# Second step of the Fourier stage: standing operands in two halves, two stores requested by ScalarE, a table load and two clears at later places

## The chip, the cores and the metric

The kernel runs on one core of a Trainium2 chip. The core has five engines with a queue of instructions each: TensorE (PE; its weight loads are listed as PEld), VectorE (DVE), ScalarE (ACT), GpSimd (POOL) and SyncE (SP, which here does little but request DMA transfers). Sixteen DMA engines move data. The metric is the time of one execution on the device in microseconds (us); the time of the kernel before is 973.52 us, the median of three runs (971.64 to 975.0).

## The reference

An encoder layer is applied to two sequences of 1024 columns, 256 and 2048 tokens long, with the same weights. Cut to what matters:

```python
def fourier_mix(u, w_f, b_f):                  # 8 groups of 64 columns
    ug = u.reshape(b, s, F_GROUPS, F_GROUP_DIM)
    spec = jnp.fft.fft2(ug, axes=(1, 3), norm='ortho')
    return spec.real.reshape(b, s, F_WIDTH) @ w_f + b_f

def encoder_layer(x, ...):
    h = rms_norm(x, g_pre)
    q, k, v, z_a, u_f, z_f = split(h @ w_in)   # six times 512 columns
    y_a = neighbourhood_attention(q, k, v, rpb)
    y_f = fourier_mix(u_f, w_f, b_f)
    mixed = concat([rms_norm(y_a, g_na) * silu(z_a),
                    rms_norm(y_f, g_f) * silu(z_f)])
    return x + rms_norm(mixed @ w_out, g_post)
```

The whole is in float32. A matrix product that needs the accuracy is made of three products of split operands, a high part and a low part (names that end in `h` and `l`); the split is a cast of the operand and a subtraction of the cast from it.

## The kernel before, in words

**Stages.** The projections come first. Their last and longest part is a loop `for i in range(16)` over pairs of output blocks, each with seven products `mm` on TensorE (lines 164 to 166). For the `z` columns the result `f` gets a silu on ScalarE (line 882) and is stored to `zD` (line 883), two stores of 512 KB for a pair. The loop's last pair, `i == 15`, is such a pair. During it SyncE also loads the constants `d2` and the first twelve `zg` tiles (line 831), the results of the Fourier stage's first step, which lie in `ZD` in DRAM.

**The Fourier stage's second step** follows (lines 982 to 1080). It runs in four rounds `gq`, each over five tiles `c`. A round reads four `zg` loads of 256 KB. Tiles 0 to 3 are `pab` products with a standing operand of 128 columns (a slice of `zg`) and 64 moving columns of `d2`, four products for a tile; tile 4 has three stripes of 32 columns side by side. In round 0 each tile has a product with one moving column as well (`pny`), and in round 2 one for the 256-token sequence (`pup`, from the loads `up` and `f256`). In the trace a float32 product is two records, so a full `pab` tile shows as eight. `split_ab` splits each result: the cast (`abh`, `a`) is on ScalarE, or on VectorE for tiles 0 to 2 of round 0, and the subtraction (`abl`) on VectorE. `pab` uses three PSUM buffers: tags `b` (two) and `c` (one). After round 2 comes a first pass `pq(0)` and after round 3 a second, `pq(1)`, and `pq32`: products `ppq` of `cs2`, `c32` with the load `wf` (1 MB), split into `pqh`, `pql` and `w32`.

**Y.** Then `py` products (lines 164 to 166 and 1263) make the mixed columns in four blocks `e`, each in three parts. ScalarE adds the bias (line 1268), VectorE combines two PSUM tiles into `Y` (line 1276) and SyncE stores `Y` (line 1302 the 256-token part, line 1325 the other, 1 MB). `Y` has two buffers, so the third block's first combination needs the first block's stores landed. Attention over the loads `kl`, `ql`, `v` and the biases `tb`, the norms, and the output projection with the weights `wo` make up the rest. `kh` is the cast of `kl` (line 1095, ScalarE), and `za` a small load of `zD` (line 1159).

**Order.** Up to `man.close()` (line 976) and for TensorE everywhere the order of the instructions is written by hand. From line 977 to the third block of `Y` a scheduler sets the order of the other engines by the waits that it foresees; `issue_after(x)` holds an instruction until `x` has been placed. Each engine then runs its queue strictly in that order.

**DMA lanes.** A request tells its completion on one of eight semaphores, `DMAHW0` to `DMAHW7` in the rows below. They are taken in turn over all requests of SyncE and ScalarE, and before a request goes out its engine waits until the last transfer of the same lane has landed.

**Small parts that the change touches.** The activation table load (line 978) follows the last silu. The clears of `ptb` (line 992), two PSUM tiles that attention uses later, open the stage on VectorE. `norm_sums` copies sums of squares out of PSUM into `nsb` on ScalarE (line 1481), eight times between 630 and 858 us.

Of the kernel before, what the change touches and what calls it, by code (L numbers as in the profile page):

```python
# [10 lines left out]
F32 = mybir.dt.float32  # L11
F32R = mybir.dt.float32r
AF = mybir.ActivationFunctionType
ALU = mybir.AluOpType
# [154 lines left out]
def build(tc, A, O):  # L169
    nc = tc.nc  # L170
# [10 lines left out]
    zD = dr.tile([2, 512, T], F32, name="zD")  # L181
# [23 lines left out]
    dnyq = cst.tile([128, 2], F32, name="dnyq")  # L205
# [11 lines left out]
    def mmt(n):  # L217
        x = mmc[0] % 5 > 2
        mmc[0] += 1
        return ps.tile([128, n], F32, tag="t" if x else "a", name="mm", bufs=2 if x else 3)  # L220
# [10 lines left out]
    def gt(shape, dtype, name):  # L231
        return gp.tile(shape, dtype, tag="g", name=name)
# [293 lines left out]
    def pair(i):  # L526
        return i if i < 8 else 15 - i
# [190 lines left out]
    for c in range(3, 6):  # L718
# [7 lines left out]
        if c == 4:  # L726
# [5 lines left out]
            for k in range(KC):  # L732
                for t in range(2):
                    ts = slice(128 * t, 128 * t + 128)
                    nc.vector.scalar_tensor_tensor(out=xp[:, k, ts], in0=xs[t][:, k], scalar=gpre[:, k:k + 1],
                                                   in1=ivb[0][:, ts], op0=ALU.mult, op1=ALU.mult)
# [23 lines left out]
    for b in range(16):  # L760
        kind, blk = divmod(b, 4)
# [12 lines left out]
        if 2 <= b < 8:  # L774
            x, y = divmod(b, 2)
# [7 lines left out]
        p = mmt(512)[:, :TP]  # L783
# [3 lines left out]
        o = st.tile([128, 256], F32, tag="f", name="f", bufs=3)  # L787
        if kind % 2:
            i, d = p, o
        else:  # L790
            i = p.rearrange("p (b r c) -> p b r c", b=2, c=32)
# [43 lines left out]
    def load_d(j):  # L835
        return load([128, 8, 128], A["d2"][:, 8 * j:8 * j + 8, :], "d2")

    zgs = []
    for i in range(16):
# [14 lines left out]
        kind, blk = divmod(2 * pair(i), 4)  # L854
        o = [st.tile([128, 1024], F32, tag="f", name="f", bufs=3) for x in range(2)]
# [23 lines left out]
        def store(f):  # L879
            ts = slice(TP + 1024 * sg, TP + 1024 * sg + 1024)  # L880
            if kind < 2:
                silu_[0] = nc.scalar.activation(o[f], o[f], AF.Silu)
                nc.sync.dma_start(zD[kind, (blk + f) * 128:(blk + f) * 128 + 128, ts], o[f])
            else:
                nc.sync.dma_start((kD if kind == 2 else qD)[blk + f, :, ts], o[f])

        silu_ = [None]
        for j in range(7):
            if i in (0, 8):
                if j in (0, 3):  # L890
# [27 lines left out]
            if sg == 0:  # L918
                x, y = divmod(7 * (pr - 1) + j, 14)
# [17 lines left out]
            for f, d in ((u_load, 0), (u_split, 4), (u_stage1, 6)):  # L937
                x = 7 * pr + j - 7 - d
# [4 lines left out]
            if i == 15 and j in (1, 3, 4, 5):  # L943
                if j == 1:
                    d2 = [load_d(0), load_d(1)]
# [4 lines left out]
            p = mmt(512)  # L950
# [5 lines left out]
            if j == 0:  # L956
                nc.scalar.copy(e_("u0"), p)
            elif j == 1:
                comb(0, 0, "u0", p)
            elif j == 2:  # L960
                add("u2", "u0")
            elif j == 3:
                add("u4", "u2")
            elif j == 4:
                comb(1, 1, "u4", p)
                add("u3", "u2")
            elif j == 5:
                comb(1, 0, "u3", p, ALU.subtract)
                store(1)
            else:  # L970
                comb(0, 1, "u4", p)
                store(0)
        if kind < 2:
            silu = silu_[0]

    man.close()
    with tc.issue_after(silu.ins):
        nc.scalar.preload_act_table_set("natural_log_exp_and_others")
    ph.close()


# [6 lines left out]
    sqs = sqp.tile([128, T], F32, name="sqs")  # L988
    ab = pf.enter_context(tc.tile_pool(name="ab", bufs=1))
    ptb = [ps.tile([128, 512], F32, tag="t", name="ptb", bufs=2) for i in range(2)]  # L990
    for x in ptb:
        nc.vector.memset(x, 0.0)
    pg = ExitStack()
    sm = pg.enter_context(tc.tile_pool(name="smF", bufs=1))
    f256 = sm.tile([128, 2, 258], F32, name="f256")
# [16 lines left out]
    a32 = ab.tile([96, NCOL], F32R, name="a32")  # L1012
    AC = [[x[:, c % 2] for x in AB[c // 2]] for c in range(4)]

    def split_ps(dh, dl, src, vec=False):
        nc.vector.tensor_copy(dh, src) if vec else nc.scalar.copy(dh, src)
        nc.vector.tensor_tensor(out=dl, in0=src, in1=dh.bitcast(F32), op=ALU.subtract)

    def dft(p, c, pairs):
        sts = [(p[32 * r:32 * r + 32], slice(256, 512, 8)) for r in range(3)] if c == 4 else \  # L1020
            [(p, slice(c * 128, c * 128 + 128))]
        for out, cols in sts:
            for x, (z, d) in enumerate(pairs):
                nc.tensor.matmul(out, z[:, cols], d, start=x == 0, stop=x == len(pairs) - 1)  # L1024


    def split_ab(gq, c, view, p):
        if c < 4:
            split_ps(view(AC[c][0]), view(AC[c][1]), p, gq == 0 and c < 3)
        else:  # L1030
            nc.scalar.copy(view(a32), p)
            lo = view(a32[64:96])
            nc.vector.tensor_tensor(out=lo, in0=p[64:96], in1=lo.bitcast(F32), op=ALU.subtract)

    def stage2(gq, zg, c):
        m = int(c in (2, 3))
        np_ = 96 if c == 4 else 128
        x = (gq * 5 + c) % 3 == 2
        p = ps.tile([np_, 4, 64], F32, tag="c" if x else "b", name="pab", bufs=1 if x else 2)
        for g in range(4):  # L1040
            dft(p[:, g, :], c, [(zg[g], d2[gq // 2][:, (gq % 2) * 4 + g, m * 64:m * 64 + 64])])
        split_ab(gq, c, lambda a: a[:, :1024].rearrange("p (k q g l) -> p q g k l", k=16, q=4, g=4)[:, gq],
                 p.rearrange("p g (k l) -> p g k l", l=4))
        if gq == 0:
            p = ps.tile([np_, 1], F32, tag="a", name="pny")
            dft(p, c, [(zg[0], dnyq[:, m:m + 1])])
            split_ab(gq, c, lambda a: a[:, 1024:1025], p)
        if gq == 2:
            p = ps.tile([np_, 129], F32, tag="a", name="pup")
            dft(p, c, [(up[:, t], f256[:, t, 129 * m:129 * m + 129]) for t in range(2)])  # L1050
            split_ab(gq, c, lambda a: a[:, 1025:1154], p)
# [4 lines left out]
    def pq(m):  # L1056
        h = gt([128, 2, 512], F32R, "pqh")
        l = gt([128, 2, 512], F32R, "pql")
        for c in range(2):
            p = ps.tile([128, 512], F32, tag="a", name="ppq")  # L1060
            for x in range(2):
                nc.tensor.matmul(p[64 * x:64 * x + 64], cs2[:, m, :], wf[:, 2 * c + x, :], start=True, stop=True)  # L1062
            split_ps(h[:, c], l[:, c], p)
        PQ.append((h, l))

    def pq32():
        p = ps.tile([96, 512], F32, tag="a", name="ppq")
        for c in range(4):
            nc.tensor.matmul(p, c32[:, c], wf[:, c], start=c == 0, stop=c == 3)
        nc.scalar.copy(w32, p)  # L1070
        nc.vector.tensor_tensor(out=w32[32:64], in0=p[32:64], in1=w32[32:64].bitcast(F32), op=ALU.subtract)

    for gq in range(4):
        for c in range(5):
            stage2(gq, zgs[gq], c)
        if gq == 2:
            pq(0)
    pq(1)
    pq32()
    pg.close()  # L1080
# [163 lines left out]
    for t, (g, x) in enumerate(zip(G, (0, 640))):  # L1244
        g["w"] = []
        for c0, w in g["t"]:
            n = 2 * g["nr"] * w
# [67 lines left out]
    for e in range(4):  # L1315
        Y = sqy.tile([128, T], F32, tag="Y", name="Y", bufs=2)
        if e < 3:
# [10 lines left out]
            for i in range(T // SQ if e < 2 else 1):  # L1328
                ts = slice(i * SQ, i * SQ + SQ)
# [146 lines left out]
    def norm_sums(sq, ts):  # L1476
        n = 32 * len(ts)
        for x, t in enumerate(ts):
            nc.tensor.matmul(ptb[0][32 * x:32 * x + 32, :128], ones32, sq[:, t * 128:t * 128 + 128], start=True, stop=True)
        o = sm.tile([128, 128], F32, name="nsb", bufs=1)[:n]  # L1480
        nc.scalar.copy(o, ptb[0][:n, :128])  # L1481
        nsb.append(o)

    def norm_turn(dst, ts):
# [89 lines left out]
    for k in range(2, len(G) + 1):  # L1574
        pr, i = divmod(k, 9)
        g, f = G[k] if k < len(G) else None, G[k - 1] if k else None
# [19 lines left out]
        x = k // 2 + 1  # L1596
# [52 lines left out]
        if k + 1 in NT:  # L1649
            norm_sums(sqs if k < 31 else ysq, NT[k + 1])  # L1650
# [8 lines left out]
        if 32 <= k < 36:  # L1659
            x, d = k - 32, atiles[k - 32]  # L1660
# [122 lines left out]
```

## Time and profile before

| | |
|---|---|
| median of three runs | 973.52 us (971.64 to 975.0) |
| the profiled execution | 970.48 us, of which the span of instructions is 968.7 us |
| granted TensorE clock in it | 0.998 |
| busy share | PE 99%, PEld 83%, DVE 73%, ACT 51%, POOL 44% |
| DMA | 279.89 MB, mean 289 GB/s |
| second step of the Fourier stage | from 549 us (first `pab`) to 576.6 us (first `py`) |

Times of the trace are microseconds from the start of the span. A row of the timeline has the start, the duration, engine, line, operation, tiles written and read, their shape and the number of merged instructions, and in brackets how long the engine stood idle before and what ended that. In a group of the profile, "busy, mean ns" are followed by the idle time before the group's instructions and what ended it. The profile's DMA share is the mean busy share of the sixteen engines. The busy share of PE counts matmuls whose ends are modelled, so 99% says that it always had something under way, not that it was at its peak.

### The profile page before, as it was taken

How to read it: one execution, taken by the hardware profiler on the slowest of the kernel's cores; microseconds unless marked ns; L12 is line 12 of the kernel's file. 1: busy time of each engine (PE TensorE's matmuls, PEld its weight loads, DVE VectorE, ACT ScalarE, POOL GpSimd, SP SyncE). 2: the span in 40 equal slices, each digit the busy share in tenths (PEclk: the TensorE clock that was granted, in tenths of full speed). 3: DMA queues.
4: the chain of work that ended last, by engine and by line, in shares of the span. 5: the costliest groups of instructions: out<-in, count | busy, mean ns of one | idle time of the engine just before them, and what ended most of it. 6: DMA issues, size and time to landing. Idle time of an engine off the chain costs nothing.

```text
span 968.7 us, 17031 instructions
## 1 busy us (share of the span) xinstructions
PE 958.9 (99%) x5769; PEld 801.0 (83%) x5769; DVE 709.5 (73%) x1306; ACT 497.5 (51%) x1078; POOL 430.2 (44%) x400
## 2 busy tenths in 40 slices
PE   9999999999999999999999999999999999999997
PEld 7889988888888888888888879887788888878886
DVE  6768987777986867787777446776665656649997
ACT  6836675433325533333344255677666776744443
POOL 3100003464752202756654033577677686624544
PEclk9999999999999999999999999999999999999999
DMA  9899696556849996599989898698887998979993
GB/s 327 312 373 357 234 366 240 194 189 252 318 163 377 352 410 239 211 371 320 322 303 339 301 328 300 210 281 273 258 240 234 286 327 270 296 244 331 330 346 129
DMA packets 146450, 279.89 MB, mean 289 GB/s; under 512 B 13162, under 2 KB 84284, under 8 KB 142972
## 3 DMA queue, kind: packets, MB, share of 16 engines
q1 hardware_dynamic: 145932, 278.41, 82.4%
q8 instruction: 46, 0.75, 0.3%
q10 hardware_dynamic: 432, 0.39, 0.1%
q14 instruction: 40, 0.33, 0.1%
HBM read 184.37 MB, written 101.72 MB: 295 GB/s over the span
## 4 chain that ended last, share of the span: by engine, by line
PE 96%; DVE 1%; ACT 1%; issue 1%; POOL 1%; DMA 0%; DVEq 0%; SPq 0%; POOLq 0%; ACTq 0%
PE po L1432 19%; PE mm L165 18%; PE mm L164 18%; PE mm L166 18%; PE pv L1521 5%; PE ptb L1505 5%; PE s L1181 4%; PE pab L1024 2%; PE py L164 1%; PE py L166 1%; PE py L165 1%; DMA gpre<-gpre 0%; PE ppq L1062 0%; PE pz L166 0%; PE pz L164 0%
## 5 line engine op out<-in xcount | busy, mean ns | idle before, releaser
L164 PE MATMUL mm<-xh,wa 128*128 128x512 f32 x448 | 174.4, 389 | 0.0
L165 PE MATMUL mm<-xl,wa 128*128 128x512 f32 x448 | 174.3, 389 | 0.0
L166 PE MATMUL mm<-xh,wa 128*128 128x512 f32 x448 | 174.3, 389 | 0.0
L536 POOL TENSOR_TENSOR ws<-wr 128x512 f32<-128x512 f32 x16 | 22.2, 1386 | 226.6 <-DMA wr<-wz 222.8
L1215 POOL TENSOR_SCALAR w<-w,m 128x480 f32<-128x480 f32 (+6 forms) x136 | 86.0, 644 | 46.3 <-DVE m L1212 35.9
L164 PEld LDWEIGHTS mm<-xh,wa 128*128 128x128 f32 x448 | 84.1, 188 | 17.6
L166 PEld LDWEIGHTS mm<-xh,wa 128*128 128x128 f32 x448 | 84.1, 188 | 17.5
L165 PEld LDWEIGHTS mm<-xl,wa 128*128 128x128 f32 x448 | 84.1, 188 | 17.4
L1432 PE MATMUL po<-wo,yh 128*128 128x512 f32 x272 | 90.4, 413 | 0.0
L551 DVE TENSOR_TENSOR wa<-wr,wa 128x512 fp32r<-128x512 f32 x60 | 68.5, 1149 | 27.1 <-ACT wa L550 26.8
L1208 ACT ACTIVATE w<-w,m 128x480 f32<-128x480 f32 (+6 forms) x136 | 79.3, 586 | 17.1 <-DVE m L1203 17.1
L1432 PE MATMUL po<-w,yh 128*128 128x512 f32 x280 | 86.7, 391 | 0.0
L1203 DVE CUSTOM_DVE_ANT_1 w<-s,tb 128x360 f32<-128x360 f32 (+5 forms) x124 | 62.4, 541 | 10.3 <-PE s L1181 9.8
L589 POOL TENSOR_TENSOR mt<-mt,rmask 128x880 f32<-128x880 f32 (+2 forms) x24 | 51.0, 2139 | 34.1 <-DVE mt L585 27.6
L165 PE MATMUL mm<-vl,xh 128*128 128x512 f32 x168 | 65.5, 390 | 0.2 <-DVE vl L482 0.2
L164 PE MATMUL mm<-vh,xh 128*128 128x512 f32 x168 | 65.4, 389 | 0.0
L166 PE MATMUL mm<-vh,xl 128*128 128x512 f32 x168 | 65.4, 389 | 0.0
L877 DVE TENSOR_TENSOR f<-u,mm 128x512 f32<-128x512 f32 x64 | 43.5, 680 | 28.0 <-PE mm L166 23.1
L1432 PEld LDWEIGHTS po<-w,yh 128*128 128x128 f32 x280 | 52.3, 188 | 10.9 <-issue 0.2
L1505 PE MATMUL ptb<-ident,w 128*120 128x128 f32 (+5 forms) x428 | 59.5, 276 | 1.0 <-ACT nsb L1481 0.9
L550 ACT CAST wa<-wr 128x512 fp32r<-128x512 f32 x60 | 36.4, 617 | 44.1 <-PE mm L166 23.2
L1521 PEld LDWEIGHTS pv<-pt,v 120*64 120x64 f32 (+6 forms) x896 | 48.2, 136 | 12.8 <-issue 9.6
(263 smaller groups left out, 2394.3 us busy)
## 6 DMA issues: line engine op xcount, KB each, us to landing
wr<-wz SPq DMA_DIRECT2D x48, 512.0 KB
vl<-sD SPq DMA_DIRECT2D x20, 512.0 KB
xm<-xm SPq DMA_DIRECT2D x9, 1024.0 KB
oD<-ofs SPq DMA_DIRECT2D x18, 512.0 KB
of<-oD SPq DMA_DIRECT2D x18, 512.0 KB
yr<-yD SPq DMA_DIRECT2D x34, 256.0 KB
zD<-f SPq DMA_DIRECT2D x16, 512.0 KB
woD<-wo SPq DMA_DIRECT2D x16, 512.0 KB
```

What stands on the lines that cost most here:

```text
L164: nc.tensor.matmul(out, lh, rh, start=first, stop=False)
L165: nc.tensor.matmul(out, lh, rl, start=False, stop=False)
L166: nc.tensor.matmul(out, ll, rh, start=False, stop=last)
L551: nc.vector.tensor_tensor(out=o[:, 1], in0=src, in1=o[:, 0].bitcast(F32), op=ALU.subtract)
L589: nc.gpsimd.tensor_tensor(out=o, in0=i, in1=rmask[:, m0:m0 + n].unsqueeze(2).to_broadcast([128, n, 80]), op=ALU.add)
L877: nc.vector.tensor_tensor(out=dst(f, b), in0=src(uu[u]), in1=src(p), op=op)
L1203: nc.vector.tensor_tensor_reduce(out=rows(g["w"][b][:, h, :n], w), in0=rows(g["s"][2 * b + h][:, :n], w), in1=tv, scale=1.0, scalar=3.0e38 ...
L1208: nc.scalar.activation(w, w, AF.Exp, bias=m[:, h:h + 1], scale=-1.0, accum_out=m[:, 2 + h:3 + h])
L1215: nc.gpsimd.tensor_scalar(w, w, m[:, 4 + h:5 + h], 1.0, ALU.mult, ALU.mult)
L1432: nc.tensor.matmul(p, (d["l"] if x == 2 else d["h"])[:, c], w(n, int(x == 1), c), start=j == 0, stop=j == 11)
L1505: nc.tensor.transpose(ptb[h][:nk, j * 128:j * 128 + 128], g["w"][b][:, h, c0:c0 + nk], ident)
L1521: nc.tensor.matmul(p[hs, b], g["v"][:nk, v, hs], g["pt"][b][:nk, h, j * 128:j * 128 + 128], start=j == 0, stop=j == len(ch) - 1)
```

## The change

Six edits, the first four in the title:

1. `dft` takes a width `w`. The `pab` and `pny` products of tiles 0 to 3 are called with 64: each standing operand of 128 columns becomes two halves of 64 columns, one after the other in the program, that write partitions 0 to 63 and 64 to 127. `pup` and tile 4 stay.
2. For `i == 15` the two stores to `zD` are requested by ScalarE, behind each silu, not by SyncE.
3. The table load moves from behind the last silu to behind the last ScalarE cast of round 3.
4. The two clears of `ptb` move to the end of round 1.
5. The cast of tile 2 in round 0 moves from VectorE to ScalarE.
6. The copy to `nsb` moves from ScalarE to VectorE.

```diff
         def store(f):
             if kind < 2:
-                silu_[0] = nc.scalar.activation(o[f], o[f], AF.Silu)
-                nc.sync.dma_start(zD[kind, (blk + f) * 128:(blk + f) * 128 + 128, ts], o[f])
+                nc.scalar.activation(o[f], o[f], AF.Silu)
+                q = nc.scalar if i == 15 else nc.sync
+                q.dma_start(zD[kind, (blk + f) * 128:(blk + f) * 128 + 128, ts], o[f])
...
     man.close()
-    with tc.issue_after(silu.ins):
-        nc.scalar.preload_act_table_set("natural_log_exp_and_others")
...
     ptb = [ps.tile([128, 512], F32, tag="t", name="ptb", bufs=2) for i in range(2)]
-    for x in ptb:
-        nc.vector.memset(x, 0.0)
...
-    def dft(p, c, pairs):
-        sts = [(p[32 * r:32 * r + 32], slice(256, 512, 8)) for r in range(3)] if c == 4 else \
-            [(p, slice(c * 128, c * 128 + 128))]
+    def dft(p, c, pairs, w=128):
+        if c == 4:
+            sts = [(p[32 * r:32 * r + 32], slice(256, 512, 8)) for r in range(3)]
+        else:
+            sts = [(p[r:r + w], slice(c * 128 + r, c * 128 + r + w)) for r in range(0, 128, w)]
...
-            split_ps(view(AC[c][0]), view(AC[c][1]), p, gq == 0 and c < 3)
+            split_ps(view(AC[c][0]), view(AC[c][1]), p, gq == 0 and c < 2)
...
-            dft(p[:, g, :], c, [(zg[g], d2[gq // 2][:, (gq % 2) * 4 + g, m * 64:m * 64 + 64])])
+            dft(p[:, g, :], c, [(zg[g], d2[gq // 2][:, (gq % 2) * 4 + g, m * 64:m * 64 + 64])], 64)
...
-            dft(p, c, [(zg[0], dnyq[:, m:m + 1])])
+            dft(p, c, [(zg[0], dnyq[:, m:m + 1])], 64)
...
     for gq in range(4):
         for c in range(5):
             stage2(gq, zgs[gq], c)
+        if gq == 1:
+            with tc.issue_after(last["dve"].ins):
+                for x in ptb:
+                    nc.vector.memset(x, 0.0)
         if gq == 2:
             pq(0)
+        if gq == 3:
+            with tc.issue_after(last["act"].ins):
+                nc.scalar.preload_act_table_set("natural_log_exp_and_others")
...
-        nc.scalar.copy(o, ptb[0][:n, :128])
+        nc.vector.tensor_copy(o, ptb[0][:n, :128])
```

**How the order changes on SyncE**, from the twelve `zg` loads on (tile numbers tell the pairs of loads apart; `zg_4771` and `zg_4774` are round 1's, `zg_4793` and `zg_4796` round 2's). Before:

```order
L831 DMA zg_4771<-ZD_70 128x512 [waits DMAHW6_49,PE_49]
L831 DMA zg_4771<-ZD_70 128x512
L831 DMA zg_4774<-ZD_70 128x512 [waits DMAHW0_49]
L831 DMA zg_4793<-ZD_70 128x512 [waits DMAHW2_49,PE_49]
L831 DMA zg_4796<-ZD_70 128x512 [waits DMAHW5_49]
L883 DMA zD_69<-f_4694 128x1024 [waits DMAHW6_49,Activation_49]
L883 DMA zD_69<-f_4693 128x1024 [waits DMAHW7_49,Activation_49]
L996 DMA f256_4859<-f256 128x516 [waits DMAHW0_49,PE_49]
L998 DMA up_4861<-uD_71 128x2x512 [waits DMAHW1_49]
```

and now:

```order
L831 DMA zg_4771<-ZD_70 128x512 [waits DMAHW0_49,PE_49]
L831 DMA zg_4771<-ZD_70 128x512 [waits DMAHW1_49]
L831 DMA zg_4774<-ZD_70 128x512 [waits DMAHW2_49]
L831 DMA zg_4793<-ZD_70 128x512 [waits DMAHW4_49,PE_49]
L831 DMA zg_4796<-ZD_70 128x512 [waits DMAHW7_49]
L989 DMA f256_4856<-f256 128x516 [waits DMAHW0_49,PE_49]
L991 DMA up_4858<-uD_71 128x2x512 [waits DMAHW1_49]
```

The two stores are gone from this queue, and the lanes have moved: in the program's new order the first store takes lane 1 and the second lane 4 ahead of the loads shown, so the second load of `zg_4771` (the sixth of twelve) waits on lane 1 for the first store, and the first load of `zg_4793` (the ninth) on lane 4 for the second.

**ScalarE at the same place.** Before:

```order
L882 ACTIVATE f<-f 128x1024 [waits DMAHW4_49,DVE_49,Activation_49]
L882 ACTIVATE f<-f 128x1024 [waits DMAHW0_49,DVE_49]
L978 ACT_TABLE_LOAD
L1016 CAST abh_4877<-pny 128x1 [waits PE_49]
L1031 CAST a_4879<-pab 96x4x16x4 [waits PE_49]
```

and now:

```order
L882 ACTIVATE f<-f 128x1024 [waits DMAHW4_49,DVE_49,Activation_49]
L884 DMA zD<-f 128x1024 [waits DMAHW1_49,Activation_49]
L882 ACTIVATE f<-f 128x1024 [waits DMAHW0_49,DVE_49]
L884 DMA zD<-f 128x1024 [waits Activation_49]
L1014 CAST abh_4874<-pny 128x1 [waits PE_49]
L1032 CAST a_4876<-pab 96x4x16x4 [waits PE_49]
```

The stores stand behind their silus (some rows of casts are left out). In round 3 the scheduler's order on ScalarE is now:

```order
L1014 CAST pqh<-ppq 128x512 [waits PE_49]
L1014 CAST abh_4872<-pab 128x4x16x4 [waits PE_49] x2
L1103 CAST kh<-kl 128x576
L1014 CAST abh_4874<-pab 128x4x16x4 [waits PE_49]
L1103 CAST kh<-kl 128x576 [waits DMAHW2_49]
L1085 ACT_TABLE_LOAD
L1032 CAST a_4876<-pab 96x4x16x4 [waits PE_49]
```

with a first `pqh` and a first `kh` ahead of these rows and another `abh` cast ahead of the table load. The table load has come between round 3's fourth and fifth tile.

**TensorE at the start of the step.** Before:

```order
L1024 MATMUL pab<-d_4717,zg 128x64 x4
L1024 MATMUL pny<-dnyq,zg 128x1
L1024 MATMUL pab<-d_4717,zg 32x64 x12
L1024 MATMUL pny<-dnyq,zg 32x1 x3
L1024 MATMUL pab<-d_4717,zg 128x64 x16
```

and now:

```order
L1025 MATMUL pab<-d_4717,zg 64x64 x8
L1025 MATMUL pny<-dnyq,zg 64x1 x2
L1025 MATMUL pab<-d_4717,zg 32x64 x12
L1025 MATMUL pny<-dnyq,zg 32x1 x3
L1025 MATMUL pab<-d_4717,zg 64x64 x32
```

Only the full tiles change, each product into two (the rows are round 0's, with its repeats left out, and round 1's).

More of the change, by code (lines that the diff above doesn't have):

```diff
@@ L881, in store @@
             if kind < 2:
-                silu_[0] = nc.scalar.activation(o[f], o[f], AF.Silu)
-                nc.sync.dma_start(zD[kind, (blk + f) * 128:(blk + f) * 128 + 128, ts], o[f])
+                nc.scalar.activation(o[f], o[f], AF.Silu)
+                q = nc.scalar if i == 15 else nc.sync
+                q.dma_start(zD[kind, (blk + f) * 128:(blk + f) * 128 + 128, ts], o[f])
             else:
                 nc.sync.dma_start((kD if kind == 2 else qD)[blk + f, :, ts], o[f])
-        silu_ = [None]
         for j in range(7):
@@ L972, in build @@
                 store(0)
-        if kind < 2:
-            silu = silu_[0]
     man.close()
-    with tc.issue_after(silu.ins):
-        nc.scalar.preload_act_table_set("natural_log_exp_and_others")
     ph.close()
@@ L1013, in build @@
     AC = [[x[:, c % 2] for x in AB[c // 2]] for c in range(4)]
+    last = {}
     def split_ps(dh, dl, src, vec=False):
-        nc.vector.tensor_copy(dh, src) if vec else nc.scalar.copy(dh, src)
-        nc.vector.tensor_tensor(out=dl, in0=src, in1=dh.bitcast(F32), op=ALU.subtract)
-    def dft(p, c, pairs):
-        sts = [(p[32 * r:32 * r + 32], slice(256, 512, 8)) for r in range(3)] if c == 4 else \
-            [(p, slice(c * 128, c * 128 + 128))]
+        if vec:
+            nc.vector.tensor_copy(dh, src)
+        else:
+            last["act"] = nc.scalar.copy(dh, src)
+        last["dve"] = nc.vector.tensor_tensor(out=dl, in0=src, in1=dh.bitcast(F32), op=ALU.subtract)
+    def dft(p, c, pairs, w=128):
+        if c == 4:
+            sts = [(p[32 * r:32 * r + 32], slice(256, 512, 8)) for r in range(3)]
+        else:
+            sts = [(p[r:r + w], slice(c * 128 + r, c * 128 + r + w)) for r in range(0, 128, w)]
         for out, cols in sts:
```

## The prediction

> **What bounds the kernel now.** I read the page first (engine shares, then the chain that ended last), then the stretch around the Fourier stage by windows, the timeline there, and the waits of SyncE's queue.
>
> ```profile
> span 968.7 us, 17031 instructions
> PE 96%; DVE 1%; ACT 1%; issue 1%; POOL 1%; DMA 0%; DVEq 0%; SPq 0%; POOLq 0%; ACTq 0%
> ```
>
> TensorE is packed and carries 96% of the chain, so a microsecond counts only if TensorE starts its later work earlier or later. The change sits at 547 to 577 us. The next rows are windows: length, busy PE, PEld, DVE, ACT, POOL, granted clock, DMA share, GB/s.
>
> ```profile
> 547.50:549.00 1.50, 1.50 (x8) 1.23 (x8) 0.00 (x0) 0.95 (x1) 0.00 (x0) 1.00 0.02 7
> 549.00:551.00 2.00, 2.00 (x20) 1.96 (x18) 1.50 (x3) 0.94 (x1) 0.00 (x0) 1.00 0.67 262
> 551.00:552.00 1.00, 1.00 (x12) 1.00 (x11) 1.00 (x6) 0.98 (x2) 0.00 (x0) 1.00 0.11 45
> 552.00:570.00 18.00, 18.00 (x219) 16.16 (x218) 10.24 (x31) 8.71 (x25) 1.41 (x1) 1.00 1.03 370
> 570.00:572.00 2.00, 2.00 (x36) 1.70 (x37) 0.55 (x2) 1.81 (x5) 0.79 (x1) 1.00 0.50 124
> 572.00:577.00 5.00, 5.00 (x17) 1.70 (x13) 2.23 (x4) 2.54 (x6) 5.00 (x5) 1.00 0.99 320
> 577.00:580.00 3.00, 3.00 (x18) 2.98 (x17) 0.68 (x1) 1.07 (x2) 1.26 (x2) 1.00 0.93 241
> 580.00:594.00 14.00, 14.00 (x82) 14.00 (x82) 7.42 (x32) 7.37 (x19) 1.66 (x3) 1.00 1.00 374
> ```
>
> DMA is nearly full from 552 to 594 with three small holes (551 to 552, 570 to 572, a little at 577 to 580). What is put off ahead of 552 is late at 594 too. Here is why there is a hole before 552, and what the loads are:
>
> ```profile
> 547.38 1.06 ACT L882 ACTIVATE f<-f 128x1024 f32<-128x1024 f32 x1 [13.79 <-DVE f L877]
> 548.47 2.98 SPq L883 DMA_DIRECT2D zD<-f  x2
> 550.05 1.06 ACT L882 ACTIVATE f<-f 128x1024 f32<-128x1024 f32 x1 [1.61 <-DVE f L877]
> 551.55 0.38 SPq L996 DMA_DIRECT2D f<-f  x1
> 556.58 1.33 SPq L1091 DMA_DIRECT2D kl<-kD  x2
> 562.79 0.34 SPq L1159 DMA_DIRECT2D za<-zD  x1
> 565.18 0.38 SPq L1135 DMA_DIRECT2D ql<-qD  x1
> ...
> zg<-ZD SPq DMA_DIRECT2D x5, 256.0 KB
> zD<-f SPq DMA_DIRECT2D x2, 512.0 KB
> ```
>
> Before the change all twelve `zg` loads of the first three rounds are requested ahead of the two stores, and DMA is empty at 547.5 to 549: they have landed. SyncE then waits for the silus and stores at 548.5 and 551.1. Store 1 (512 KB) is done about 551, 2.5 us after its request, by the windows. Of three loads the landing is seen in the request eight further, which waits for it: `up` 556.6 (`kl`), `wf` 562.8 (`za`), `kl` 565.2 (`ql`).
>
> **The halves.** The pace of stage 2 on TensorE:
>
> ```profile
> L1024 PEld LDWEIGHTS pab<-d,zg 128*128 128x128 f32 x128 | 15.1, 192 | 1.0 <-PE ppq L1062 0.8
> ...
> 553.58 0.59 PEld L1024 LDWEIGHTS pab<-d,zg 128*32 128x32 f32 x24
> 560.02 0.97 PEld L1024 LDWEIGHTS pab<-d,zg 128*128 128x128 f32 x8
> 565.40 1.94 PE L1062 MATMUL ppq<-wf,cs 128*64 128x512 f32 x8
> 567.26 4.44 PE L1024 MATMUL pab<-d,zg 128*128 128x64 f32 x56
> 573.51 3.67 PE L1069 MATMUL ppq<-wf,c 128*96 128x512 f32 x8
> 576.62 0.74 PE L164 MATMUL py<-abh,pqh 128*128 128x386 f32 x1
> ```
>
> A full tile is eight records, (0.97 − 0.192)/7 = 111 ns apart, about 0.89 us. Three 32-column stripes side by side (the stripe tile, 24 records) take 0.59 us. No row has two 64-column halves with 64 moving columns: the bounds are 0.59 us a tile (they run side by side as the stripes do) and 2 x 0.97 us (each half costs a full load, one after the other). I take 0.59, the nearest form. 16 tiles x 0.30 = −4.8 us of TensorE time, with `pny` about −5. It counts only where nothing else holds TensorE.
>
> The Trainium skill speaks against this, "TensorE: Matmul & The Clock Gate", Part 3: a weight load overlaps a running matmul only when the row groups differ, and halves of columns share all rows. By that the −4.8 would be 0. The stripes share all rows too, and their 24 loads fit in 0.59 us, 25 ns each, so the trace does not bear the rule out for columns.
>
> **The stores on ScalarE.** The order rows of SyncE show the cost. Requests take eight completion lanes in turn, in the program's order, and each waits until the request eight back has landed. Store 1 now holds lane 1 and store 2 lane 4, so `zg` load 6 waits for store 1 to land and load 9 for store 2, and everything behind them on SyncE's queue (five more `zg`, `f256`, `up`, the last `zg` four, `cs2`, `c32`, `wf`, `kl`, `tb`, `wo1`, `Y`) stands still too. Before, all of them passed ahead of the stores or right after their request. ScalarE pays two requests:
>
> ```profile
> L619 ACTq DMA_DIRECT2D xr<-xt x2: 412/432/451, 0.7 to 1.2; - x2
> ```
>
> 0.43 us each, beside idle time of ScalarE (1.61 us between the silus): 0.
>
> Store 1 goes out at 548.5 as before and lands at 551.1 or a bit later. Loads 6 to 8 are then requested, and share DMA with store 2 (out at 551.1) until 555.7; store 2 lands about 555, loads 9 to 12 begin to move about 1.1 us after that. Seven loads x 262 KB / 370 GB/s = 5.0 us of transfers that ran before 547.5 now stand ahead of `f256`; the hole while load 9 waits adds 0 to 0.4, a late piece of store 1 would let store 2 finish sooner and take off 0.2. So `f256` to `kl` and `wo1` land 4.8 to 5.4 us later: `up` about 561.6, `wf` about 567.8, `kl` about 570.2.
>
> **Table load, clears, casts, nsb.** Durations, and where they go:
>
> ```profile
> L1016 ACT CAST abh<-pab 128x256 fp32r<-128x256 f32 x13 | 4.8, 372 | 7.1 <-PE pab L1024 5.9 <-issue 1.2
> L1017 DVE TENSOR_TENSOR abl<-pab,abh 128x256 fp32r<-128x256 f32 x16 | 6.8, 423 | 6.9 <-ACT abh L1016 6.9
> L1095 ACT CAST kh<-kl 128x576 fp32r<-128x576 f32 x4 | 2.6, 677 | 0.0
> L1016 ACT CAST pqh<-ppq 128x512 fp32r<-128x512 f32 x4 | 2.3, 586 | 1.0 <-PE ppq L1062 1.0
> L978 ACT ACT_TABLE_LOAD x1 | 1.3, 1283 | 0.0
> L992 DVE MEMSET ptb<- 128x512 f32 x2 | 1.0, 485 | 0.2
> ...
> L1481 ACT COPY nsb<-ptb x8: 247/260/261, 630.0 to 858.1; 128x128 f32<-128x128 f32 x6, 64x128 f32<-64x128 f32 x2
> ...
> PE ptb L1505 <- ACT nsb L1481: 0.9, 1, 0.9
> ```
>
> The two clears leave the start of the stage (−0.97 us for VectorE) and fall after round 1, where VectorE waits for late loads: 0. The cast of tile 2 goes from VectorE to ScalarE (0.37) in round 0, ahead of the wait for load 6: 0. The table load leaves the place right behind the second silu (551.1), where no cast of ScalarE is due yet, for round 3, where ScalarE has the most to do; it is in the chain below. `nsb` on VectorE: it removes at best the one TensorE wait of 0.9 and can at worst put 8 x 0.1 in its place; I take −0.3, range −0.9 to +0.8.
>
> **Sum, step by step.** Round 0 ends about 553; TensorE then waits for loads until 555.8, again for load 12 (559) and `up` (561.6); round 2 is done about 565.5 and TensorE waits for `wf` until 568 (565.40 before): here the halves have bought nothing. `ppq` of pass 0 ends at 569.9. Round 3 needs 2.5 us on TensorE by the halves, but tile 3 needs tile 0's buffer, which ScalarE frees after `pqh` 0.59, `kh` 0.68 (`kl` at 570.2), `pqh` 0.59, `abh` 0.37 and VectorE's 0.42: 572.3. Tile 4 follows at 572.7, `ppq` of pass 1 from 573.2 (1.9), then 3.1 to 578.2: the first `py` comes 1.6 us late (576.62 before). The table load and casts end at 579.9, just ahead of the matmul that needs `w`. Then the Y rows:
>
> ```profile
> 585.41 0.33 SPq L1325 DMA_DIRECT2D yD<-Y  x1
> 594.21 1.34 DVE L1276 TENSOR_TENSOR Y<-t,py 128x252 f32<-128x252 f32 x7 [2.00 <-DMA yD<-Y]
> 596.44 0.34 PE L164 MATMUL py<-abh,pqh 128*128 128x384 f32 x1
> ```
>
> The 1 MB store of the first `Y` goes out at 585.4 but lands at 594.1 behind the `wo1` loads; the third `Y` takes its buffer, so VectorE stood 2.0 us, and frees at 595.55 the PSUM buffer that TensorE wants at 596.44: slack 0.9. With the queue 4.8 to 5.4 late, less 0.2 to 0.5 of hole, that store lands at 598.4 to 599.4, the buffer is free at 599.8 to 600.8: TensorE is 3.4 to 4.4 late there, the 1.6 included. DMA share falls after 594, so nothing more is added. +3.9 − 0.3 = +3.6; I take +3.4, since TensorE's waits give the queue a little room in `wo1`. The profiled execution is 970.48 (span 968.7), 3.0 below the median of the runs, 973.52; so 973.9 in the profile and 976.9 as median. About 0.3% (2.9 us) is what a measurement here can tell from none.
>
> **Rivals.**
> - Faster: the held loads do no harm, because the stores land early enough. From `wf` landing before 563.5 and the `Y` store before 595, TensorE keeps up to −5 us of halves, `nsb` −0.3: 968.2 to 970. For it: SyncE's 5 us of waiting for silus is gone. Against: seven loads behind a store that ends at 551.
> - Absorbed: the queue makes up most of the delay in `wo1` and `Y` lands at most 1.5 to 3 us later: +0 to +2, 973.5 to 975.5. For it: SyncE's requests there partly wait for TensorE. Against: DMA share 0.93 to 1.00.
> - Clock: TensorE waits of 2.1 to 2.8 us three times, and the end of the trace shows what an idle TensorE gets:
>
> ```profile
> 962.00:965.00 3.00, 0.00 (x0) 0.00 (x0) 2.70 (x11) 1.00 (x6) 1.44 (x2) 0.92 0.46 173
> 965.00:968.70 3.70, 0.00 (x0) 0.00 (x0) 0.65 (x1) 0.00 (x0) 0.00 (x0) 0.50 0.39 145
> ```
>
>  Half clock came some 2.6 us after its last work. Half speed on some 3.4 us of matmuls after the `Y` wait costs 1.7 more: 978.6. The Trainium skill, same page, Part 1, has the clock drop after an idle window of about 3.4 us; by that alone these waits would be too short.
> - The halves do not run side by side: nothing changes until `wf` comes; round 3 costs 0 to 4 us more, of which the `Y` wait covers 2: 976.5 to 978.9.
>
> **Chances.** Forecast as summed 0.54 (own range 975 to 979; 0.39 slower, 0.15 within 0.3%), faster rival 0.15, absorbed 0.15 (0.13 same, 0.02 faster), clock 0.08 (slower), serial halves 0.08 (0.05 slower, 0.03 same). Faster 0.17, same 0.31, slower 0.52. The range runs from the middle of the faster rival, 969.0, to above the clock's, 979.5.
>
> **What would show it.** SyncE's sixth `zg` request not before 551 and the ninth about 555, idle TensorE before rounds 1 and 2 and before `ppq`, `za` requested near 567.8, pab tiles of 0.6 us in round 3, the table load in round 3, VectorE's first combination of the third `Y` at 598 or later with a longer wait for the `Y` store, and TensorE idle there. I am wrong if SyncE requests load 6 at once, or if `wf` comes late but the `Y` store does not.

## The result, and the profile after

The changed kernel takes 978.39 us (median of 7 runs, 975.56 to 983.18), the kernel before 973.35 us in the same runs. The ratio is 1.0059, 95% interval 1.0036 to 1.0081: slower by 5 us. The profiled execution took 975.56 us. The page of it (span, busy shares, and the chain by engine):

```profile
span 973.8 us, 17305 instructions
PE 958.1 (98%) x5905; PEld 797.9 (82%) x5905; DVE 705.9 (72%) x1312; ACT 496.7 (51%) x1072; POOL 430.9 (44%) x400
PE 92%; DMA 5%; DVE 1%; issue 1%; POOL 1%; SPq 0%; ACT 0%; DVEq 0%; POOLq 0%; ACTq 0%
```

The chain had 96% PE and no DMA; now 5% of it is DMA. Its longest pieces in order of time (start, length, what) say which transfers:

```profile
551.23 2.66 DMA zD<-f
554.31 4.15 DMA zg<-ZD
558.48 7.74 DMA zg<-ZD
566.24 10.42 DMA ql<-qD
580.02 10.85 DMA wo<-woD
590.96 8.87 DMA yD<-Y
```

From the second store (551) to the landing of the first `Y` store (600) the end of the kernel hangs on transfers and, from 576.7 to 580.0, on SyncE's requests for the next of them. What SyncE's queue and TensorE wait for, in the view of the waits (us in total, times, longest):

```profile
SPq L831 <- DMA zD<-f: 13.2, 2, 13.0
...
PE pab L1025 <- DMA zg<-ZD: 3.1, 3, 2.0
PE pup L1025 <- DMA up<-uD: 1.6, 1, 1.6
...
PE py L164 <- DVE Y L1284: 0.7, 1, 0.7
...
PE ptb L1513 <- DVE nsb L1489: 0.6, 1, 0.6
PE pab L1025 <- DVE abl L1015: 0.5, 1, 0.5
```

SyncE's requests for `zg` stood 13.0 us, until a store that was not yet requested had gone out and landed. TensorE, which before waited for nothing in this stage, waits 3.1 us for `zg` and 1.6 for `up`. The timeline has the places (rows picked):

```profile
548.56 0.34 ACTq L884 DMA_DIRECT2D zD<-f  x1
549.31 0.69 PE L1025 MATMUL pab<-d,zg 128*64 128x64 f32 x16
552.34 3.35 SPq L831 DMA_DIRECT2D zg<-ZD  x7
555.06 0.48 PE L1025 MATMUL pab<-d,zg 128*64 128x64 f32 x4 [2.01 <-DMA zg<-ZD]
563.54 0.96 SPq L1099 DMA_DIRECT2D kl<-kD  x2
569.44 0.34 SPq L1167 DMA_DIRECT2D za<-zD  x1
570.63 1.94 PE L1063 MATMUL ppq<-wf,cs 128*64 128x512 f32 x8
570.88 0.38 SPq L1143 DMA_DIRECT2D ql<-qD  x1
580.76 0.74 PE L164 MATMUL py<-abh,pqh 128*128 128x386 f32 x1
599.95 2.34 DVE L1284 TENSOR_TENSOR Y<-t,py 128x252 f32<-128x252 f32 x10 [3.59 <-DMA yD<-Y]
601.44 0.41 PE L164 MATMUL py<-abh,pqh 128*128 128x384 f32 x1 [0.68 <-DVE Y L1284]
```

The seven held loads go out one after the other from 552.3 to 555.7. `up` lands at 563.5 (556.6 before), `wf` at 569.4 (562.8), the first `py` starts at 580.8 (576.6), the first `Y` store lands at 600 (594), and the product that needs the freed buffer starts at 601.44 (596.44): 5.0 us late, and the span is 5.1 us longer. A full `pab` tile is 16 records in 0.69 us where it was 8 in 1.00: the halves do run side by side. The row of the kernel before is

```profile
549.14 1.00 PE L1024 MATMUL pab<-d,zg 128*128 128x64 f32 x8
```

Windows of the changed kernel (length, busy PE, PEld, DVE, ACT, POOL, granted clock, DMA share, GB/s):

```profile
551.00:552.20 1.20, 1.09 (x40) 1.04 (x39) 0.91 (x5) 0.59 (x4) 0.00 (x0) 1.00 0.17 68
555.00:557.00 2.00, 0.97 (x8) 0.59 (x8) 0.00 (x0) 0.00 (x0) 0.00 (x0) 0.50 0.87 288
562.00:563.60 1.60, 0.07 (x4) 0.01 (x1) 0.97 (x3) 0.37 (x1) 0.00 (x0) 1.00 1.06 394
566.00:568.50 2.50, 2.50 (x30) 2.15 (x28) 0.90 (x3) 0.72 (x3) 0.00 (x0) 0.50 0.98 399
568.50:570.00 1.50, 1.50 (x39) 1.31 (x37) 0.66 (x3) 0.64 (x2) 0.00 (x0) 0.96 1.04 414
```

DMA stands nearly empty until 552.2 (a share of 0.17 from 551.0 on, 0.26 in the kernel before), while SyncE waits for the first store's last pieces. The granted clock falls to half after the wait of 2.0 us, comes back, and falls again after the wait of 1.6 us at 562.

### The profile page after: what moved, and what is told of

It is laid out like the page before. It is cut to its first block, busy times and chain, and to the rows that moved or that the text cites. A ratio compares the mean times of both kernels' runs of the same rounds, so it can differ in the third digit from the quotient of the medians.

```text
span 973.8 us, 17305 instructions
## 1 busy us (share of the span) xinstructions
PE 958.1 (98%) x5905; PEld 797.9 (82%) x5905; DVE 705.9 (72%) x1312; ACT 496.7 (51%) x1072; POOL 430.9 (44%) x400
## 4 chain that ended last, share of the span: by engine, by line
PE 92%; DMA 5%; DVE 1%; issue 1%; POOL 1%; SPq 0%; ACT 0%; DVEq 0%; POOLq 0%; ACTq 0%
PE po L1440 20%; PE mm L165 18%; PE mm L166 18%; PE mm L164 18%; PE pv L1529 5%; PE ptb L1513 5%; PE s L1189 4%; DMA zg<-ZD 1%; DMA wo<-woD 1%; DMA ql<-qD 1%; DMA yD<-Y 1%; DMA gpre<-gpre 0%; PE pz L166 0%; PE pz L165 0%; PE pz L164 0%
```

## The experiments

Theory 1: the loss is the hold of loads by the stores' lanes, and the gain of the halves is capped by the queue up to the first `Y` store. Theory 2: the hold is the loss and nothing caps the halves. Theory 3: the halves, the later table load or the stores on another engine cost by themselves.

All milestones below are from the traces, in us from the first `pab` matmul, so that differences ahead of the stage drop out ("attention" is the first product `s` of line 1181 in the kernel before; "end" the last instruction).

| kernel | first ppq | first py | attention | end | time, ratio to before (95%) |
|---|---|---|---|---|---|
| before | 16.3 | 27.5 | 50.7 | 419.6 | 1 |
| changed | 21.3 | 31.5 | 55.6 | 424.5 | 1.0059 (1.0036 to 1.0081) |
| e1 stores on SyncE | 14.9 | 25.0 | 50.2 | 419.4 | 0.9992 (0.9979 to 1.0004) |
| e2 before, stores on ScalarE | 28.2 | 39.7 | 62.9 | 432.9 | 1.0125 (1.0103 to 1.0147) |
| e3 before, halves | 15.6 | 25.7 | 50.6 | 419.4 | 0.9995 (0.9982 to 1.0008) |
| e5 stores on GpSimd | 14.6 | 24.7 | 50.1 | 420.6 | 0.9997 (0.9985 to 1.0009) |
| e6 e2, waits filled | 22.1 | 33.4 | 57.5 | 427.4 | 1.0074 (1.0057 to 1.0091) |
| e7 changed, waits filled | 20.7 | 30.8 | 56.0 | 426.3 | 1.0068 (1.0049 to 1.0086) |
| e8 e1, four wo1 later | 15.0 | 25.1 | 48.4 | 421.1 | 1.0011 (0.9999 to 1.0022) |
| e9 e8, wf earlier | 13.0 | 23.8 | 47.1 | 418.8 | 0.9995 (0.9983 to 1.0007) |
| e10 stores behind the loads | 15.3 | 26.6 | 54.1 | 423.0 | 1.0039 (1.0024 to 1.0054) |
| e11 e10, wf earlier | 12.5 | 23.8 | 56.5 | 426.2 | 1.0053 (1.0038 to 1.0069) |
| e12 e11, four wo1 later | 12.5 | 23.4 | 48.1 | 422.0 | 1.0034 (1.0020 to 1.0049) |

**e1: the changed kernel, the stores back on SyncE.**

```diff
-                q = nc.scalar if i == 15 else nc.sync
+                q = nc.sync
```

> The changed kernel with one edit undone: SyncE requests the last pair's stores again, so no zg load stands behind a store. Theory 1 (the hold of the loads is the loss, and the DMA queue up to the first Y store caps the gain of the halves): pace of pab tiles 0.6 us, wf lands at 562 to 563 as in the kernel before, ppq starts at 563 instead of 565.4, py at 573 to 574 instead of 576.6, but the first Y store lands at 594 as before, so TensorE waits for VectorE's first combination of the third Y some 2.5 us: net -0.5 to -1.5 us, 972 to 973. Theory 2 (the hold is the loss and nothing else limits): the halves reach the end, -4 to -5 us, 968.5. Theory 3 (the halves themselves, the later table load or the clock cost): 976 to 979, TensorE still late at py.

Measured 971.69 against 972.53. The 5 us are gone with this one edit, so the other five cost nothing that can be seen; theory 3 falls for them. Theory 2 falls too: the halves bring the first `py` 2.5 us forward, but attention only 0.6. TensorE's waits in the profile of e1:

```profile
PE py L164 <- DVE Y L1284: 1.7, 1, 1.7
PE ppq L1063 <- DVE a L1034: 1.6, 1, 1.6
...
PE pup L1025 <- DMA up<-uD: 0.6, 1, 0.6
...
PE pab L1025 <- DVE abl L1015: 0.5, 1, 0.5
PE pv L1529 <- DMA v<-vD: 0.4, 1, 0.4
```

They sum to 4.8 us, all new, and take back most of what the halves save: from the first `pab` to the first `py` TensorE is busy for 22.1 us, against 27.5 in the kernel before. The 1.6 ahead of `ppq` ends where `wf` lands: it is put down to the last semaphore that the profile shows.

**e2: the kernel before with the stores on ScalarE alone.**

```diff
-                nc.sync.dma_start(zD[kind, (blk + f) * 128:(blk + f) * 128 + 128, ts], o[f])
+                q = nc.scalar if i == 15 else nc.sync
+                q.dma_start(zD[kind, (blk + f) * 128:(blk + f) * 128 + 128, ts], o[f])
```

> The kernel before with one edit alone: ScalarE requests the two stores of the last pair. Theory 1 (the loads held behind the stores are the whole loss): zg loads wait for the stores, wf at 568 to 570, first Y store at 599 to 600, +4 to +6 us, 977.5 to 979.5, a little more than the changed kernel because whole tiles run at 0.89 us or slower behind late loads. Theory 3 (other edits cost): within 0.3% of before, 972 to 975.

Measured 984.97 against 972.53: +12.4, more than twice what theory 1 gave. The windows of e2 show what was missing from it (the clock is the third number from the end):

```profile
557.00:560.00 3.00, 1.15 (x6) 1.01 (x6) 0.00 (x0) 0.18 (x1) 0.00 (x0) 0.73 0.96 277
560.00:575.00 15.00, 15.00 (x90) 14.71 (x91) 4.27 (x11) 3.60 (x11) 0.00 (x0) 0.50 1.03 396
580.00:585.00 5.00, 5.00 (x62) 4.44 (x60) 2.57 (x5) 3.73 (x9) 2.04 (x2) 1.00 0.91 320
```

After a wait of 1.85 us for `zg` TensorE gets half the clock and keeps it for some 20 us (558.4 to 578.9), although it is busy throughout once the wait is over: the whole tiles, with weight loads under way for 14.7 of 15 us, do not bring it back. A full tile takes 1.81 us there, and TensorE is the bound of the stage again.

**e3: the kernel before with the halves alone** (`w=64` in the two calls of `dft`, nothing else).

> The kernel before with one edit alone: halves of 64 columns. If they run side by side, 16 pab records of a tile take 0.6 us instead of eight in 0.9. Theory 1 (the DMA queue up to the first Y store caps it): py 2 to 3.5 us earlier, TensorE waits at the third Y for the store, net -0.5 to -1.2 us, 972.3 to 973. Theory 2 (nothing caps): -4 to -5 us, 969. If the halves cost: slower.

Measured 972.13 against 972.53, much as theory 1 had it: no difference that can be measured, with the first `py` 1.8 us earlier (just short of its 2 to 3.5) and attention 0.2.

**e5: the changed kernel, the stores on GpSimd.**

```diff
-                q = nc.scalar if i == 15 else nc.sync
+                q = nc.gpsimd if i == 15 else nc.sync
```

> The changed kernel with GpSimd instead of ScalarE requesting the last pair's stores; in the program GpSimd's requests use completion semaphores of their own, so no load of SyncE waits for a store, and SyncE does not wait for the silus either. Theory 1: zg all land by 548.5, f256 goes out at about 549.5 instead of 551.5, wf lands at 560.5 to 562, the first Y store at 592 to 593.5, TensorE waits for it less: -2 to -4 us, 969.5 to 971.5. Theory 3 (moving the stores off SyncE costs by contention, not by the hold): 976 to 979.

Measured 972.64 against 972.53: no hold of `zg`, no loss; but not the gain that I expected. Two long waits of SyncE in e5:

```profile
SPq L989 <- PE mm L166: 5.6, 1, 5.6
SPq L1099 <- DMA zD<-f: 4.9, 1, 4.9
```

With the stores out of the way `f256` waits 5.6 us for the projections' last matmul, whose operands lie in its memory. It still goes out earlier, 0.1 us after the first `pab` against 2.4 in the kernel before. But `wf` lands later, 14.5 us after the first `pab` against 13.7, and `kl` waits for the store: GpSimd's two stores take 6.5 us from request to landing in the median, beside these loads. That they are what slows `wf` is not shown.

**e6 and e7: TensorE's waits filled.** Products of `ident` with itself, 0.22 us each, into a PSUM tile that nobody reads, at the places where TensorE waits for loads: in e6 in e2's kernel, in e7 in the changed one.

```diff
+            if (gq, c) == (1, 0):
+                keep((0, 2, 1, 8)[g])            # e7: (0, 8, 1, 3)
             dft(p[:, g, :], c, ...)
...
         if gq == 2:
+            if c == 0:
+                keep(10)                         # e7: 6
```

> The kernel of e2 (stores on ScalarE alone) with matmuls that nobody reads, 128 moving columns each, put where TensorE waits for loads: 2, 1 and 8 inside the first tile of round 1, 10 ahead of the first pup. If the half clock that the waits bring on is what costs e2 more than the late loads: the granted clock stays near 1.0, ppq starts at 571 to 573 instead of 578, +4 to +6 us against before, 977 to 979. If the late loads alone make the +12 (waits for each load, no matter the clock): it stays at 983 to 986.

> The changed kernel with the same filling of TensorE's waits (8, 1 and 3 matmuls in the first tile of round 1, 6 ahead of the first pup). In the changed kernel the stage at half clock ended at 570.6, when wf had been there since 569.4: if the clock costs only what lies beyond the load, -0.5 to -1.5 us against the changed kernel, 977 to 978. If the clock costs more (also in what follows): 974 to 976. If the clock has nothing to do with it or the filling delays the tiles: 978.5 to 980.

e6: 979.49, 5.5 us below e2, and its window says that the clock stayed:

```profile
560.00:570.00 10.00, 10.00 (x109) 9.87 (x108) 4.16 (x11) 3.45 (x11) 0.00 (x0) 1.00 1.04 385
```

So of e2's 12.4 us some 5.5 are the half clock and 6.8 the late loads. The same whole tiles that do not bring the clock back in e2 do not lose it here. e7: 979.07, no better than the changed kernel (978.39), although `ppq` comes 0.6 us earlier; the wait at the third `Y` grows from 0.7 to 1.7 us. So in the changed kernel the half clock lies inside the wait for loads. That is what the halves are good for there: they carry the stage through the half clock, and the changed kernel takes 6.6 us less than e2, while on time they are worth nothing.

**e8 and e9: what caps the halves.** In e8 four of the eight `wo1` loads are requested behind the first `Y` store; in e9 also round 3's `zg` behind `wf`.

```diff
-    for n in range(2): ...                   # wo1 loads, n = 0 and 1
+    wo_get(0)
...
             nc.sync.dma_start(yD[1, e, :, TP:], Y[:, TP:])
+            if e == 0:
+                wo_get(1)
```

> The kernel of e1 (all edits but the stores, which SyncE requests) with the last four wo1 loads requested behind the first Y store, not ahead of it. If the queue ahead of that store caps the gain: the store lands some 5 us earlier, the 1.7 us wait of TensorE at the third Y is gone, -1.5 to -2.5 us against before, 970 to 971. If something else holds TensorE there (VectorE and ScalarE in the scheduler's order, or wo1 being late for the output projection): no change against e1, 971.5 to 973.

> e8 and also the zg loads of round 3 requested behind wf, not ahead of it. wf then lands about 2.7 us earlier (560 to 561) and the 1.6 us wait of TensorE for it ahead of the first ppq goes; round 3's loads land at 563, when ppq ends: -3 to -4 us against before, 968.5 to 969.5. If round 3 waits for its loads instead, or for kl's casts: as e8, 970 to 971.

973.5 and 972.45 against 972.71: no gain that can be measured, both above the ranges given for them. The wait for the first `Y` store is gone and attention starts 2.4 and 3.7 us earlier than in the kernel before, but the end does not. TensorE's waits in e8 behind that point:

```profile
PE ptb L1517 <- DVE pt L1521: 1.0, 1, 1.0
...
PE ptb L1517 <- POOL ql L1172: 0.5, 1, 0.5
...
PE po L1444 <- ACT y0h L1362: 0.5, 1, 0.5
```

And the window of e8 from 606 us on:

```profile
606.00:640.00 34.00, 31.96 (x237) 24.71 (x237) 24.00 (x80) 22.05 (x63) 18.79 (x27) 0.95 0.67 215
```

GpSimd, VectorE and ScalarE at the start of attention did not come earlier by as much as TensorE, and in e8 its waits there cost clock as well (0.95 of the window, against 1.00 before and in e9). The cap of theory 1 is real, but only the first of several.

**e10 to e12: ScalarE's stores without a hold of zg.** Each store waits for the last `zg` load to land; in e11 `wf` is also requested ahead of round 3's loads; e12 is e11 with e8's `wo1`.

```diff
+                if i == 15:
+                    tc.add_manual_dep(st_.ins, zl[0].ins.name, ...)   # zl[0]: the last zg load
```

> The changed kernel, with ScalarE still requesting the two stores, but each made to wait for the last of the twelve zg loads to land. In the program's order the stores then take lanes 0 and 4 behind the loads, and the requests that wait for them are wf's and kl's, no zg load. The scheduler puts the first store and the second silu behind the casts of round 1. If the loss is the hold of the zg loads through the lanes: TensorE has no wait for zg, the first py comes 24.5 to 27 us after the first pab (31.5 in the changed kernel), 971 to 974.5, as with the stores on SyncE. If it is ScalarE's requests as such, or the stores' transfers beside the loads: 976 to 979 as in the changed kernel.

> e10 with wf, cs2 and c32 requested ahead of round 3's four zg loads, so that only the last of these and kl wait for a store's lane. wf then needs no store landed: wf at 558 to 560, first ppq 12 to 13.5 us after the first pab (16.3 in the kernel before, 15.3 in e10), first py 22.5 to 25. If the later waits (first Y store, VectorE's and ScalarE's work ahead of attention) take what comes early, as in e1 and e8: 971 to 973.5. If the hold of wf was all that kept the gain of the halves from the end: 968 to 970.

> e11 with the last four wo1 loads behind the first Y store as in e8: TensorE reaches attention 3 to 5 us earlier than in the kernel before (46 to 48 us after the first pab, 50.7 before). If ScalarE, VectorE and GpSimd ahead of attention give back what TensorE gains, as in e8 and e9: 971 to 973.5. If there is nothing behind it: 968 to 970.

e10 missed its time: 975.36 against 972.51, between both. No `zg` waits and rounds 0 to 2 run through, but the scheduler put the first store at 555.9, and now `wf` stands behind it, as SyncE's timeline of e10 has it, and then TensorE's:

```profile
554.00 0.33 SPq L1002 DMA_DIRECT2D c<-c  x1
559.90 0.33 SPq L1004 DMA_DIRECT2D wf<-wf  x1
...
564.68 3.40 PE L1069 MATMUL ppq<-wf,cs 128*64 128x512 f32 x8 [2.70 <-issue]
```

In e11 it is the last `zg` load, and all behind it, in SyncE's timeline:

```profile
553.78 11.16 SPq L833 DMA_DIRECT2D zg<-ZD  x4
565.71 0.80 SPq L1105 DMA_DIRECT2D kl<-kD  x2
```

And the longest of TensorE's waits in e11:

```profile
PE py L164 <- DVE Y L1290: 5.5, 1, 5.5
```

There the first `py` is 3.7 us earlier than in the kernel before and the kernel is 5.3 us slower (977.78 against 972.48): the whole lead and more is waited off at the third `Y`. Part of the loss is the clock, which falls behind that wait. Two windows of e11, then e10's (the clock is the third number from the end):

```profile
594.00:606.00 12.00, 6.46 (x25) 6.16 (x24) 3.62 (x16) 3.08 (x8) 4.60 (x7) 0.77 0.76 280
606.00:612.00 6.00, 6.00 (x44) 5.07 (x43) 3.54 (x20) 3.50 (x12) 0.70 (x1) 0.89 0.44 175
...
594.00:606.00 12.00, 9.55 (x52) 8.92 (x51) 5.47 (x30) 5.09 (x15) 5.71 (x8) 0.86 0.69 263
```

e11 works at half clock for 6.2 us behind its wait of 5.5 us, e10 for 3.4 behind one of 2.5: by my estimate, half of these times, 3.1 of e11's 5.3 us and 1.7 of e10's 2.8. e1 has two waits of 1.6 and 1.7 us at full clock and loses nothing.

e12 shortens the wait at the third `Y` to 0.4, but then TensorE waits 2.9 us for `y0h` and loses clock behind that; 976.03. Both e11 and e12 came out above every range given for them. So the loss moves with the hold, in part by way of the clock; e10 to e12 do not separate the two. That the transfers beside the loads or ScalarE's requests cost by themselves, as e10's other reading had it, is not excluded by these times, but the longest of TensorE's waits in e10 and e11 are for what stood behind a store or follows from it.

No version beats the kernel before by more than can be measured; the nearest is e1.

## Why the prediction was right

The forecast was 976.9 us, slower, and 978.39 came out (+5.0 against +3.4). By its steps:

- **The hold.** Right: load 6 waits for store 1, the queue behind stands, and the delay goes through `up`, `wf`, `kl` and `wo1` to the first `Y` store. e1 shows that this edit is the whole loss.
- **Its size** was the term that came out too small: 4.8 to 5.4 us were forecast, `up` was 7.0 late, `wf` 6.7, `kl` (seen in `ql`'s request, 570.88 against 565.18) 5.7. I took store 1 as landed 2.5 us after its request, from the DMA share. The request that waits for it went out 3.8 us after it (548.56 to 552.34): the share shows when most of the bytes are through, and a waiting request goes by the last piece. That this put the queue back by as much is not shown: in e7 store 1 took 4.4 us, and `up` came only 0.2 later, counted from the store's request. What the windows show is that more moved ahead of `up` than I had counted: from 552 us to its landing 1.57 MB before (4.58 us at 343 GB/s) and 3.98 MB now (11.54 us at 345), 2.4 MB more at the same rate, where the sum had the seven loads, 1.8 MB. Which requests the rest belongs to stays open.
- **The halves.** Side by side, as taken from the stripes (16 records in 0.69 us on PE and 0.55 on PEld). The 0.59 that I took was the stripes' whole length, set against a pace of 0.89; by pace the halves do better, three tiles in 1.60 us in e1's round 3. The 5.4 us that TensorE is busy for less in e1 compare with about 5 in the sum. The rival of serial halves falls. The Trainium skill's rule ("TensorE: Matmul & The Clock Gate", Part 3, overlap of a weight load with a running matmul only where row groups differ) is not borne out here: sixteen loads with the same rows take 0.55 us on PEld, where eight whole ones took 0.97.
- **The first py** was to be 1.6 late and was 4.1: the larger delay, and half clock in round 2, where `pup` took 1.23 us. TensorE was to stand idle for `wf` ahead of `ppq`; it did not, since it was still in round 2 when `wf` landed at 569.4, and `ppq` began at 570.6.
- **The Y store.** Right as to place: it landed at 600 (forecast 598.4 to 599.4) and freed the buffer at 601.3. With `py` itself 4.1 late only 0.7 us of wait was left of it.
- **The clock** was a rival at 0.08, placed behind the `Y` wait. It fell earlier, with waits of 2.0 and 1.6 us, shorter than the 2.6 that I had read at the end of the trace. Length alone does not decide it: two waits of 1.9 us in e5 left it at 1.00. It cost nothing here that e7 can show, but 5.5 us without the halves (e2 and e6). The forecast had not weighed that the halves would cover it, so this part came out by luck. By the Trainium skill's figure for the idle window (same page, Part 1, about 3.4 us) neither wait would have brought it on.
- **The faster rival** was mispriced: with the loads on time I gave the halves -5 us. e1 and e3 have them on time and measure -0.8 and -0.4, both within the interval of no change.
- **Table load, clears, casts:** together 0, as forecast (e1 has them and e3 does not: ratios 0.9992 and 0.9995); none was tried alone. The `nsb` wait went from 0.9 to 0.6 us, the -0.3 of the sum.

## What to carry to other kernels

Moving a transfer to another engine's queue takes its waiting off one queue, but where requests share completion semaphores in turn, the request eight further inherits it; read the waits of the built program before such a move. Ahead of a faster matmul stage, ask which transfer and which other engine its followers need next: here 5.4 us of TensorE time saved came back as 4.8 us of waits. A wait of TensorE in a stage of small matmuls costs more than its length when it halves the clock.

## What the hardware showed that was not expected

- Half the granted clock with waits of only 1.6 to 2.0 us (the changed kernel, e2), but not with two of 1.9 us in e5. It then lasted 20.5 us in e2, with TensorE busy on tiles of 64 moving columns to a 128-column load; in the changed kernel, with halves, the clock was back after 6.8 us and then after 3.4.
- In the traces' records of the clock every stretch at half clock in the stages shown here lasts 3.41 us or a whole multiple: 3.41 in e8, e10 and e12, 6.83 in e11, 6.83 and 3.41 in the changed kernel, 20.48 in e2. Whether the place of a wait against such steps decides if the clock falls was not tried.
- A 512 KB store with DMA otherwise nearly empty: most of its bytes through 2.5 us after the request, but the request that waits for its landing goes out 3.8 us after (4.0 in e2, 4.4 in e6 and e7).
